# The convolution module over ctx in steps beside the first layer's feed-forward part, and modulation rows beside both attentions

## The chip, the cores and the metric

The kernel runs on one core of a Trainium2 chip. The metric is the device time of one execution in microseconds, lower is better. The engines are named as in the profile: PE is TensorE's matmul, PEld its weight load, DVE is VectorE, ACT is ScalarE, POOL is GpSimd, SP is SyncE, which here only issues DMAs.

## The reference

Two blocks follow one another, in float32. The first has two layers over x (512 tokens, 1024 features): a latent attention and a stick-breaking attention of 4 heads each, whose outputs are merged under sigmoid gates, and a feed-forward part with 2816 hidden features and a causal convolution of width 3. The second block has two layers over x and over ctx (256 tokens): a conformer convolution module in the first, an attention with axial rotary positions in the second, and a gated feed-forward part in each. ctx enters only in the second block, and nothing of x flows into it before the attention. Each layer is modulated by vectors that come from a condition.

```python
def first_block(x, c, ...):
    for l in range(2):
        mod = silu(c) @ w_ada[l] + b_ada[l]            # six vectors of 1024
        h = rms_norm(x, g_norm1[l]) * (1 + sc1) + sh1
        u = h @ w_in[l] + b_in[l]                      # q, kv, stick q k v, two gates
        merged = sigmoid(gate_mla) * (y_mla @ w_branch_mla[l]) + sigmoid(gate_sb) * (y_sb @ w_branch_sb[l])
        x = x + gt1 * (merged @ w_out[l])
        h = rms_norm(x, g_norm2[l]) * (1 + sc2) + sh2
        a, v = split(causal_conv3(h @ w_up[l]))
        x = x + gt2 * ((silu(a) * v) @ w_down[l])

def conv_module(h, ...):
    a, gt = split(h @ w_pw1 + b_pw1)
    u = depthwise_conv31(a * sigmoid(gt)) + b_dw
    return silu(layernorm(u, ln_g, ln_b)) @ w_pw2 + b_pw2

def second_block(x, c, ctx, c_ctx, ...):
    for i in range(2):
        mod_x, mod_c = silu(c) @ w_mod[i] + b_mod[i], silu(c_ctx) @ w_mod[i] + b_mod[i]
        hx, hc = rmsnorm(x) * (1 + sc_x) + sh_x, rmsnorm(ctx) * (1 + sc_c) + sh_c
        yx, yc = conv_module(hx), conv_module(hc)      # i = 0; the attention where i = 1
        x, ctx = x + g_x * rmsnorm(yx), ctx + g_c * rmsnorm(yc)
        x = x + gf_x * rmsnorm(swiglu(rmsnorm(x) * (1 + scf_x) + shf_x))      # ctx the same where i = 0
```

## The kernel before, in words

Arrays are feature-major: 8 tiles of 128 features by the tokens. Every product of float32 matrices is made of three passes over parts that a tensor engine format holds exactly: hi x hi, lo x hi and hi x lo (`dense`, lines 184 to 186). Weights arrive as chunks of 128 x 1024. `weights` (lines 158 to 169) loads one over SP's queue into `raw`, ACT copies the hi part to `whi` (L165), and DVE takes the difference as `wlo` (L168), or POOL does for every `lo_pool`-th chunk. Each of the three has a ring of three buffers. One chunk is 24 matmuls of 512 columns for x, or of 256 for half of x or for ctx.

A modulation row (`modulation_rows`, lines 292 to 313) makes 128 outputs of a vector times a matrix: a DMA of 512 KB, one DVE instruction of 1024 elements that multiplies with the row of the condition (`crow`, for ctx `ccrow`) and accumulates (L308), and a small read of the accumulator. It either takes its buffer from the ring of `raw` and throws its product into the ring of `whi`, or has buffers of its own where a pool is handed over. Rows run in steps: `side_work(n)` (line 146) takes n steps from a generator where the program calls it, next to a chunk's matmuls.

The order of instructions on each engine is fixed when the program is built, by a scheduler that follows the program roughly and moves what is ready. Each engine then runs its queue in order.

The stages of `first_layer` (from line 667), for each of the two layers: the latent attention; the stick attention's queries, keys (`stick_rows`) and values (`stick_values`); its heads, beside 16 `gate` products (L184 to L186 into `g`); 16 `gated` products (L663: gate times the branch product `br`), the second 8 of which are merged and split (L285); the output projection in halves; the feed-forward part in three parts of 8, 7 and 7 hidden tiles, each an `up` stretch (L740 to L752) and a `dn` stretch (L778), the last one in halves of 256 tokens. In layer 0 the attention has 32 rows of its own second half of modulation, one per step of the products from the stick queries on, and the feed-forward part 48 rows for layer 1. Layer 1's attention has none, and its feed-forward part has 48 rows of the second block's matrix, each against two vectors (96 DVE instructions); ctx is loaded and normed there (`start_ctx`, `ctx_norm`).

`conv_layer` (line 885) then has the gating products of ctx (8 tiles, `glu`, 16 chunks) and of x (16 chunks). The 31-wide convolution over ctx is on DVE: one ACT instruction and 30 DVE taps of 256 elements per tile (L929), 12 taps per ctx tile and 15 at two places per x tile. The convolution over x is on PE: each tile is copied by 16 DMAs into shifted copies (`shifted`) and multiplied by 32 small matrices (L948, `cv`). Layer norms and the second products (`back`) follow, ctx's between those of x; `between` starts the next feed-forward part with ctx between the two halves' norms. That part, `ffn2` (line 840), runs in six parts of 4, 4, 4, 3, 3 and 4 hidden tiles over x and ctx. The tiles with names that end in c or begin with ctx are ctx's.

## Time and profile before

| | us |
|---|---|
| runs, median of 3 (lowest, highest) | 3262.71 (3258.6, 3264.51) |
| span of the profiled execution, first to last instruction | 3256.1 |
| PE busy | 3045.2 (94%) |
| DVE busy | 2118.7 (65%) |
| ACT busy | 1378.8 (42%) |
| POOL busy | 818.3 (25%) |
| 622 copies of hi parts, ACT | 599.0 |
| 433 differences for lo parts on DVE, 189 on POOL | 503.2 and 467.0 |
| HBM read and written | 402.81 and 2.10 MB |

The profile is of one execution, and the span is all that it tells of that execution's time. Busy times are sums over the whole span; the stages differ, and the windows below show them apart. The stages in the trace: attention of layer 0 from 66, its output projection from 366, its feed-forward part from 412 to 788; the same of layer 1 from 817, 1113 and 1160 to 1563; the convolution layer from 1563, with ctx's gating products to 1627, x's loop to 1823, norms, and the second products to 1937; the feed-forward part after it to 2500.

### The profile page before, as it was taken

The page shows a single profiled execution, that of the slowest core. Times are in us where ns is not written, and L with a number is a line of the kernel's source. Part 1 is how long each engine was busy: PE and PEld are TensorE (multiplying, and loading weights), DVE is VectorE, ACT ScalarE, POOL GpSimd, SP SyncE. Part 2 cuts the span into 40 slices and gives each one's busy share as a digit, 9 for nine tenths or more (in the row PEclk, how much of TensorE's full clock was granted, in tenths as well). Part 3 has the DMA queues.
Part 4 walks back from the last instruction along what each step waited for, and adds up shares of the span by engine and source line. Part 5 has one row for each costly group of instructions (what it writes and reads, how often), then busy time and mean ns, then how long its engine had stood idle before and what let it go on. Part 6 is the DMA issues. An engine that isn't in the chain of part 4 may idle for free. (4 is left out here: it accounts for less than half of the span.)

```text
span 3256.1 us, 45125 instructions
## 1 busy us (share of the span) xinstructions
PE 3045.2 (94%) x16916; PEld 2554.5 (78%) x16916; DVE 2118.7 (65%) x3863; ACT 1378.8 (42%) x2523; POOL 818.3 (25%) x618
## 2 busy tenths in 40 slices
PE   6999999999999999999899789999998789999997
PEld 5776888888777787877856589888887667898887
DVE  7654775657543688888997786544549976672326
ACT  4535552335534562324513564222235556553223
POOL 4000223233000222223555352000025621240023
PEclk9999999999999999999999889999999989999998
DMA  6442445654221355554434345333434310243323
GB/s 239 135 138 95 136 168 190 192 179 150 90 72 49 123 174 175 170 188 131 146 111 119 104 136 175 98 110 130 138 106 139 119 44 14 75 143 111 94 97 117
DMA packets 129322, 416.69 MB, mean 128 GB/s; under 512 B 16208, under 2 KB 21840, under 8 KB 129104
## 3 DMA queue, kind: packets, MB, share of 16 engines
q1 hardware_dynamic: 123984, 404.96, 38.5%
q10 hardware_dynamic: 3072, 4.43, 0.5%
q0 software_dynamic: 2048, 4.43, 0.5%
q8 instruction: 133, 2.18, 0.3%
q14 instruction: 85, 0.70, 0.1%
HBM read 402.81 MB, written 2.10 MB: 124 GB/s over the span
## 5 line engine op out<-in xcount | busy, mean ns | idle before, releaser
L165 ACT CAST whi<-raw 128x1024 fp32r<-128x1024 f32 (+4 forms) x622 | 599.0, 966 | 1008.8 <-PE dn L185 299.9
L168 POOL TENSOR_TENSOR wlo<-raw,whi 128x1024 fp32r<-128x1024 f32 (+3 forms) x189 | 467.0, 2472 | 1275.0 <-ACT whi L165 1237.4
L168 DVE TENSOR_TENSOR wlo<-raw,whi 128x1024 fp32r<-128x1024 f32 (+4 forms) x433 | 503.2, 1163 | 284.3 <-ACT whi L165 276.8
L184 PE MATMUL dn<-hi,whi 128*128 128x256 f32 (+1 forms) x1088 | 363.5, 338 | 19.8 <-DVE x L778 13.5
L186 PE MATMUL dn<-hi,wlo 128*128 128x256 f32 (+1 forms) x1088 | 361.5, 336 | 7.6 <-DVE wlo L168 7.5
L185 PE MATMUL dn<-lo,whi 128*128 128x256 f32 (+1 forms) x1088 | 364.5, 336 | 1.7 <-DVE lo L285 1.5
L184 PE MATMUL up<-hh,whi 128*128 128x512 f32 (+1 forms) x800 | 292.1, 367 | 7.2 <-ACT hh L269 7.2
L185 PE MATMUL up<-hl,whi 128*128 128x512 f32 (+1 forms) x800 | 292.5, 366 | 0.3 <-DVE hl L270 0.2
L186 PE MATMUL up<-hh,wlo 128*128 128x512 f32 (+1 forms) x800 | 291.7, 365 | 0.0
L308 DVE SCALAR_TENSOR_TENSOR mjunk<-mraw,crow 128x1024 f32<-128x1024 f32 (+1 forms) x176 | 224.0, 1273 | 39.9 <-PE g L185 21.1
L184 PEld LDWEIGHTS dn<-hi,whi 128*128 128x128 f32 x1088 | 207.3, 191 | 47.9 <-issue 14.0
L186 PEld LDWEIGHTS dn<-hi,wlo 128*128 128x128 f32 x1088 | 206.9, 191 | 32.5 <-DVE wlo L168 9.9
L185 PEld LDWEIGHTS dn<-lo,whi 128*128 128x128 f32 x1088 | 208.8, 192 | 25.0 <-DVE lo L285 2.3
L860 DVE TENSOR_TENSOR s<-s,pv 128x512 f32<-128x512 f32 (+1 forms) x76 | 41.0, 539 | 283.7 <-PE pv L186 278.0
L184 PE MATMUL pa<-hh,whi 128*128 128x512 f32 (+1 forms) x496 | 179.5, 362 | 6.2 <-ACT whi L165 3.4
L185 PE MATMUL pa<-hl,whi 128*128 128x512 f32 (+1 forms) x496 | 178.8, 361 | 2.8 <-DVE hl L270 2.7
L186 PE MATMUL pa<-hh,wlo 128*128 128x512 f32 (+1 forms) x496 | 178.0, 359 | 2.0 <-DVE wlo L168 2.0
L184 PEld LDWEIGHTS up<-hh,whi 128*128 128x128 f32 x800 | 152.4, 191 | 31.4 <-ACT hh L269 7.7
L185 PEld LDWEIGHTS up<-hl,whi 128*128 128x128 f32 x800 | 152.4, 191 | 24.5 <-DVE hl L270 0.8
L186 PEld LDWEIGHTS up<-hh,wlo 128*128 128x128 f32 x800 | 152.3, 191 | 23.8
L186 PE MATMUL pv<-hh,wlo 128*128 128x512 f32 (+1 forms) x432 | 152.7, 353 | 0.2 <-POOL wlo L168 0.2
L184 PE MATMUL pv<-hh,whi 128*128 128x512 f32 (+1 forms) x432 | 152.5, 353 | 0.0
(471 smaller groups left out, 7427.7 us busy)
## 6 DMA issues: line engine op xcount, KB each, us to landing
raw<-in_w SPq DMA_DIRECT2D x148, 512.0 KB, 3.4
raw<-in_w_up SPq DMA_DIRECT2D x100, 512.0 KB, 3.5
mraw<-in_w_modt SPq DMA_DIRECT2D x96, 512.0 KB, 3.6
mraw<-in_w_adat SPq DMA_DIRECT2D x80, 512.0 KB, 3.4
raw<-in_w_pw SPq DMA_DIRECT2D x56, 512.0 KB, 3.5
raw<-in_w_down SPq DMA_DIRECT2D x48, 448.0 KB, 3.5
raw<-in_w_g SPq DMA_DIRECT2D x32, 512.0 KB, 3.2
raw<-in_w_out SPq DMA_DIRECT2D x32, 512.0 KB, 3.6
```

The source lines that it names most:

```text
L165: nc.scalar.copy(hi[:, :n], raw[:, :n])
L168: eng.tensor_tensor(lo[:, :n], raw[:, :n], hi[:, :n], op=ALU.subtract)
L184: mm(out, lhsT=hi[:, k, :], rhs=xh[:, cols], start=(k == 0), stop=False)
L185: mm(out, lhsT=hi[:, k, :], rhs=xl[:, cols], start=False, stop=False)
L186: mm(out, lhsT=lo[:, k, :], rhs=xh[:, cols], start=False, stop=(k == n - 1))
L308: behind(nc.vector.scalar_tensor_tensor(junk, raw, 1.0, v, op0=ALU.mult, op1=ALU.mult, accum_out=d[:, f : f + 1]))
L860: nc.vector.tensor_tensor(s, s, pv, op=ALU.mult)
```

## The change

Rows: `side_work` takes two steps in the stick values, gates and gated products, so layer 0's attention holds 80 rows (its own 32 and the 48 for layer 1) and layer 1's attention 80 more (`second_mods`: 48 of the second block for x, then, with `crow` reloaded from a row parked in DRAM, 32 for ctx). The other 16 rows for ctx run in layer 0's feed-forward part. Rows of the second block are loaded once for x and once for ctx, 48 loads more in all. All these rows use the rings of `raw` and `whi`.

ctx: `ctx_conv` is a generator that loads ctx and runs its whole convolution module beside layer 0's feed-forward part, one step per hidden tile or `dn` product: 24 weight chunks, the 240 taps (now L983), the norm before and the layer norm; its output goes to DRAM (`parked`). Layer 1's feed-forward part loads ctx and that output again (`late`) and makes the two norms after the module. `conv_layer` has only x left. ctx's first four hidden tiles of the next feed-forward part are made in it (`fill`): one before x's loop, one before its last convolution, two between the layer norms of the halves. POOL takes no lo parts there any more.

```diff
@@ stick_values, gate, gated
-        core.side_work(1)
+        core.side_work(2)
...
@@ first_layer
-            core.side_work(100)
...
             if part == 0:
-                next_mod(fp)
+                steps = beside(fp)
...
-                core.side_work(2)
-                if k1 == NF and i == k0 + 4:
-                    core.side_work(100)
-                    early()
+                next(steps, None)
             last = k1 == NF
+            if last:
+                for _ in steps:
+                    pass
...
                     else:
-                        core.side_work(1)
+                        next(steps, None)
...
+def ctx_conv(core, fp, T, st, mod_steps, parked):
...
+    for k in range(KD):
+        nc.sync.dma_start(out=T.x[k], in_=a["ctxT"][k])
+    for n in range(EARLY_MODS):
+        for _ in range(-(-16 // EARLY_MODS)):
+            next(mod_steps, None)
+        yield
...
+    for k in range(KD):
+        st.squares(core, T.x[k], k)
+    pre_norm(core, st, 0, norm_gain(core, 0, 0))
+    yield
+    taps = (15,) + tuple(j for j in range(31) if j != 15)
+    for m in range(KD):
+        u = fp.tile([P, C + 30], F32, tag="uc", name="uc", bufs=3)
+        glu(core, lambda: fp.tile([P, S], F32, tag="up", name="sgc", bufs=4), st, m, u, core.at_psum)
+        yield
+        for n, j in enumerate(taps):
+            src = u[:, j : j + C]
+            if n == 0:
+                nc.scalar.activation(T.y[m], src, AF.Identity, bias=core.col("b_dw", m), scale=wdv[:, m, 15:16])
+            else:
+                nc.vector.scalar_tensor_tensor(T.y[m], src, wdv[:, m, j : j + 1], T.y[m], op0=ALU.mult, op1=ALU.add)
+            if n in EARLY_TAPS:
+                yield
+        summed(core, T.y, total, m)
+    layer_norm(core, mean_mat, st, total)
+    yield
+    for m in range(KD):
+        pointwise_back(core, st, m, core.at_psum, squares=False)
+        nc.gpsimd.dma_start(out=parked[m], in_=T.y[m])
+        if m % 2:
+            yield
...
@@ conv_layer
-        core.lo_pool = CONV_LO
-        core.side = taps_dve(us)
-        for m in range(KD):
-            u = up.tile([P, C + 30], F32, tag="uc", name="uc", bufs=KD)
-            glu(T, m, u)
-            us.append(u)
-            core.side_work(CONV_C)
+        next(fill, None)
         ready = []
...
-            core.side_work(CONV_X)
             ready.append(shifted(m, u))
-            if m == KD - 1:
-                back(T)
             if len(ready) > CONV_AHEAD:
                 taps_pe(m - CONV_AHEAD, *ready.pop(0))
-            core.side_work(CONV_X)
...
+        next(fill, None)
         for r in ready:
...
-        pre(T)
-        layer_norm(A, total)
-        between()
-        layer_norm(B, total)
+        layer_norm(core, mean_mat, A, total)
+        for _ in fill:
+            pass
+        layer_norm(core, mean_mat, B, total)
...
@@ emit
-                core.side = core.modulation_rows(a["w_adat"][0], [crow], bias0, [mod], [48], 16)
+                core.side = chain(core.modulation_rows(a["w_adat"][0], [crow], bias0, [mod], [48], 16),
+                                  core.modulation_rows(a["w_adat"][1], [crow], core.colrange("b_ada1"), [mods[1]], [48]))
...
+            def second_mods():
+                yield from mod_rows(0, [crow], [modx[0]], [48])
+                nc.sync.dma_start(out=crow, in_=parked_row.partition_broadcast(P))
+                yield from mod_rows(0, [crow], [modc[0]], [48], 16)
...
+            def late(fp):
...
                 for k in range(KD):
                     nc.sync.dma_start(out=T.x[k], in_=a["ctxT"][k])
+                    nc.sync.dma_start(out=T.y[k], in_=parked[k])
+                for _ in range(LATE_STEPS):
+                    yield
                 for k in range(KD):
+                    st.squares(core, T.y[k], k)
+                yield
+                post_norm(core, st, 2, norm_gain(core, 0, 1))
+                yield
+                T.h = halves_of(T.room(F32R))
+                pre_norm(core, st, 3, norm_gain(core, 0, 2))
...
+            def fill():
+                for f in range(NBUF2):
+                    ffn2_up(core, None, 0, f, [st], {"c": made[f]})
+                    if f in FILLS:
+                        yield
```

Places in the order of instructions. The first is DVE in layer 0's attention, among the gated products of the second branch (`br` is the product, `gate` the gate's tile, `lo` half of the merged tile's split, `wlo` the next chunk's lo part). Before:

```order
L663 TENSOR_TENSOR gate<-gate,br 128x512
L168 TENSOR_TENSOR wlo<-raw,whi 128x512
L285 TENSOR_TENSOR lo<-gate,hi 128x256 x2
L663 TENSOR_TENSOR gate<-gate,br 128x512
L168 TENSOR_TENSOR wlo<-raw,whi 128x512
L285 TENSOR_TENSOR lo<-gate,hi 128x256 x2
```

The same place in the change, where `mjunk` and a column of `mod` are a row's outputs:

```order
L308 SCALAR_TENSOR_TENSOR mjunk,mod_106<-mraw,crow 128x1024
L285 TENSOR_TENSOR lo<-gate,hi 128x256 x2
L308 SCALAR_TENSOR_TENSOR mjunk,mod_106<-mraw,crow 128x1024
L663 TENSOR_TENSOR gate<-gate,br 128x512
L168 TENSOR_TENSOR wlo<-raw,whi 128x512
L308 SCALAR_TENSOR_TENSOR mjunk,mod_106<-mraw,crow 128x1024
L285 TENSOR_TENSOR lo<-gate,hi 128x256 x2
```

Two rows have come between one gated product and the next; PE's order is the same in both kernels here.

The second is DVE at the first `dn` stretch of layer 0's feed-forward part (`dn` is the down product, `x_78` and so on x's tiles). Before, with one row per product:

```order
L308 SCALAR_TENSOR_TENSOR mjunk,mod_106<-mraw,crow 128x1024 x2
L778 SCALAR_TENSOR_TENSOR x_78<-dn,mod_105,x_78 128x512
L308 SCALAR_TENSOR_TENSOR mjunk,mod_106<-mraw,crow 128x1024
L778 SCALAR_TENSOR_TENSOR x_79<-dn,mod_105,x_79 128x512
L168 TENSOR_TENSOR wlo<-raw,whi 128x1024
L308 SCALAR_TENSOR_TENSOR mjunk,mod_106<-mraw,crow 128x1024
L778 SCALAR_TENSOR_TENSOR x_80<-dn,mod_105,x_80 128x512
```

In the change (`uc` is a gated tile of ctx, `early_4514` the output tile that its taps sum into):

```order
L778 SCALAR_TENSOR_TENSOR x_78<-dn,mod_105,x_78 128x512
L168 TENSOR_TENSOR wlo<-raw,whi 128x1024
L907 SCALAR_TENSOR_TENSOR uc<-pa,cols,sgc 128x256
L168 TENSOR_TENSOR wlo<-raw,whi 128x1024
L983 SCALAR_TENSOR_TENSOR early_4514<-uc,wdv,early_4514 128x256 x7
L778 SCALAR_TENSOR_TENSOR x_79<-dn,mod_105,x_79 128x512
L983 SCALAR_TENSOR_TENSOR early_4514<-uc,wdv,early_4514 128x256 x9
```

Runs of taps have taken the place of the rows, and the chunks of the module's own products add their lo parts.

The third is PE at the end of layer 1's feed-forward part, where the convolution layer begins (`pa`, `pg` gating products, `ctx_hl` ctx's normed input). Before, ctx's gating products follow the last `dn`:

```order
L184 MATMUL dn<-hi,whi 128x256
L185 MATMUL dn<-lo,whi 128x256
L186 MATMUL dn<-hi,wlo 128x256
L184 MATMUL pg<-ctx_hl,whi 128x256
L185 MATMUL pg<-ctx_hl,whi 128x256
L184 MATMUL pa<-ctx_hl,whi 128x256
```

In the change one hidden tile of ctx's next feed-forward part (`pv`, and a `pa` before it, 48 matmuls) and the last norm's small matmuls (`rb`) stand between it and x's gating products over 512 columns (`hh_86`, x's normed input):

```order
L185 MATMUL pv<-ctx_hl,whi 128x256
L238 MATMUL rb<-mean_col,acc 128x1
L238 MATMUL rb<-mean_col,sqx 128x1
L238 MATMUL rb<-mean_col,acc 128x1
L238 MATMUL rb<-mean_col,sqx 128x1
L186 MATMUL pv<-ctx_hl,wlo 128x256
L243 MATMUL rb<-ident,rs_y 128x128 x2
L184 MATMUL pg<-hh_86,whi 128x512
```

The 384 matmuls of ctx's gating that stood here have gone to layer 0's feed-forward part.

## Rows read from the trace of the kernel before

**Rows 1.** Stage windows: us, busy PE, PEld, DVE, ACT, POOL, clock, DMA share, GB/s.

```profile
66.00:366.00 300.00, 289.40 (x1265) 223.69 (x1264) 174.84 (x392) 143.25 (x340) 23.85 (x29) 0.99 0.37 121
...
412.00:788.00 376.00, 370.56 (x1916) 316.50 (x1915) 244.77 (x377) 156.01 (x228) 120.42 (x67) 0.99 0.54 177
...
817.00:1113.00 296.00, 285.71 (x1264) 221.78 (x1263) 139.59 (x325) 140.67 (x330) 21.68 (x31) 1.00 0.23 72
...
1160.00:1563.00 403.00, 378.97 (x1926) 321.39 (x1924) 340.30 (x510) 164.05 (x249) 124.44 (x69) 0.97 0.53 169
1563.00:1627.00 64.00, 53.24 (x390) 51.84 (x391) 62.87 (x100) 30.26 (x46) 35.70 (x34) 0.89 0.40 134
...
1823.00:1873.00 50.00, 31.75 (x211) 29.43 (x212) 43.66 (x122) 32.87 (x73) 17.07 (x15) 0.76 0.28 85
1873.00:1937.00 64.00, 55.29 (x434) 54.54 (x433) 51.67 (x100) 41.78 (x85) 31.53 (x20) 0.90 0.50 163
```

**Rows 2.** Waits, whole span: who, for whom: us in total, times, longest.

```profile
PE dn L184 <- DVE x L778: 13.5, 5, 6.9
```

**Rows 3.** DVE's groups by shape: count, busy us, mean ns, idle before.

```profile
L168 DVE TENSOR_TENSOR wlo<-raw,whi 128x1024 fp32r<-128x1024 f32 x309 | 394.5, 1278 | 220.8 <-ACT whi L165 217.1
L308 DVE SCALAR_TENSOR_TENSOR mjunk<-mraw,crow 128x1024 f32<-128x1024 f32 x144 | 184.7, 1283 | 6.7 <-DMA mraw<-in_w_modt 5.4 <-DMA mraw<-in_w_adat 0.9
L929 DVE SCALAR_TENSOR_TENSOR yc<-uc,wdv,yc 128x256 f32<-128x256 f32 x240 | 127.6, 598 | 0.7 <-ACT yc L927 0.7
...
L308 DVE SCALAR_TENSOR_TENSOR mjunk<-mraw,ccrow 128x1024 f32<-128x1024 f32 x64 | 87.4, 1365 | 1.0
...
L308 DVE SCALAR_TENSOR_TENSOR mjunk<-mraw,crow 128x1024 fp32r<-128x1024 f32 x32 | 39.3, 1228 | 33.2 <-PE g L185 21.1 <-PE qk L185 5.0 <-PE sbv L194 4.7
...
L308 DVE DVE_READ_ACCUMULATOR mjunk<-mraw,crow 128x1 f32 x176 | 14.4, 82 | 0.0
```

**Rows 4.** Windows, the last stick heads and the gated products of both layers.

```profile
331.00:366.00 35.00, 34.57 (x151) 27.58 (x150) 25.91 (x45) 20.07 (x45) 12.90 (x13) 1.00 0.32 101
1078.00:1113.00 35.00, 34.54 (x151) 27.53 (x150) 25.88 (x45) 20.17 (x45) 16.25 (x21) 1.00 0.41 131
...
292.00:331.00 39.00, 34.43 (x125) 22.34 (x123) 16.46 (x37) 21.22 (x47) 0.00 (x0) 0.96 0.19 61
```

**Rows 5.** DMA issues, whole span: queue, count, KB each, us to landing.

```profile
mraw<-in_w_adat SPq DMA_DIRECT2D x80, 512.0 KB, 3.4
...
raw<-in_w_br SPq DMA_DIRECT2D x32, 256.0 KB, 2.8
```

**Rows 6.** Windows in which one kind of matmul fills PE.

```profile
1877.00:1901.00 24.00, 24.00 (x202) 24.00 (x201) 19.70 (x29) 19.50 (x38) 11.50 (x6) 1.00 0.55 174
1300.00:1350.00 50.00, 50.00 (x221) 41.10 (x220) 38.78 (x52) 17.20 (x22) 13.01 (x6) 1.00 0.51 169
1762.00:1769.00 7.00, 7.00 (x65) 2.04 (x58) 5.62 (x12) 6.35 (x13) 6.18 (x8) 1.00 0.37 83
```

**Rows 7.** Groups of ACT by shape: a load of its function tables.

```profile
L751 ACT ACT_TABLE_LOAD x1 | 1.3, 1283 | 0.0
```

**Rows 8.** Timeline of PE, before layer 1: start, us, instruction, idle before.

```profile
787.93 0.28 PE L186 MATMUL dn<-hi,wlo 128*128 128x256 f32 x1
...
805.52 0.74 PE L192 MATMUL lat<-whi,hh 128*128 128x448 f32 x1 [1.66 <-ACT hh L269]
```

**Rows 9.** Timeline of PE, layer norms of the convolution layer.

```profile
1832.31 0.56 PE L238 MATMUL rb<-mean_col,acc 128*128 128x1 f32 x2 [9.66 <-DVE acc L221]
...
1839.44 0.69 PE L243 MATMUL rb<-ident,rs_y 128*128 128x128 f32 x2 [3.38 <-DVE rs_y L210]
```

**Rows 10.** Timelines of DVE, then of POOL, in the stretch of ctx's taps.

```profile
1602.07 7.93 DVE L929 SCALAR_TENSOR_TENSOR yc<-uc,wdv,yc 128x256 f32<-128x256 f32 x10
...
1611.06 0.47 DVE L929 SCALAR_TENSOR_TENSOR yc<-uc,wdv,yc 128x256 f32<-128x256 f32 x1
...
1606.65 2.67 POOL L168 TENSOR_TENSOR wlo<-raw,whi 128x1024 fp32r<-128x1024 f32 x1 [2.62 <-ACT whi L165]
```

More of the change, by code (lines that the diff above doesn't have):

```diff
@@ L1 @@
 from contextlib import ExitStack
+from itertools import chain
 import numpy as np
@@ L845, in ffn2 @@
         first, last = part == 0, part == len(parts) - 1
-        hid = {b.tag: [core.pair(fp, b.n, "hid" + b.tag, nbuf) for _ in range(k0, k1)] for b in bases}
+        hid = {b.tag: made[b.tag] if first and b.tag in made else
+               [core.pair(pools[b.tag], b.n, "hid" + b.tag, nbuf) for _ in range(k0, k1)] for b in bases}
         core.lo_pool = 2 if first or last else 0
@@ L882, in ffn2, with conv_layer @@
             yield
-    core.lo_pool = 0
-def conv_layer(core, X, A, B, T, post, pre, between):
+def conv_layer(core, X, A, B, post, pre, fill):
     nc, a, tc = core.nc, core.a, core.tc
-    ob1 = COLS["b_pw1"][0]
     UW = S + 32
```

246 lines of the change are left out of this document (123 added, 123 removed).

## The prediction

> **What bounds the kernel now.** I read the windows by stage first. TensorE (PE) is busy over 90% of both attentions and both feed-forward parts, VectorE (DVE) much less, except in the second feed-forward part, where DVE reaches 340.3 of 403 us (84%) [rows 1]. So PE sets the pace, and what differs between the stages is how often it waits. Two pairs of windows price such waits: the two attentions do the same work, with 32 modulation rows in the first and none in the second (300 and 296 us), and the two feed-forward parts do the same matmuls with 48 and with 96 row instructions (376 and 403 us) [rows 1]. The chain from 1563 to 1937 holds the convolution layer; in its norms, 1823 to 1873, PE is busy 31.75 of 50 us at a granted clock of 0.76 [rows 1]. Outside the norms PE's largest wait for DVE comes to 13.5 us in the whole span [rows 2]: today DVE hardly holds PE up, and a stage that gets more DVE work has room for such waits to appear.
>
> **The change, part by part.** PE's work hardly changes: the 24 chunks of ctx leave one stage and enter another. What changes is what DVE does beside it, and the waits.
>
> *A. Gated products.* A row is a DVE instruction of 1228 ns and the read of its accumulator, 82 ns [rows 3]: 1.31 us. Both layers now have two rows per step. In order, from the split of the last stick head on, 21 rows stand among the DVE work of the last 12 gated products, where none stood. That stretch took 35 us in each layer, PE busy 34.5 and DVE 25.9 [rows 4]. With 21 x 1.31 = 27.5 more, DVE has 53.4 us to do in order, and each gated product waits for a split or a product behind a row: 53.4 - 35 = +18 per layer, **+37**. Bounds: if half the rows drifted ahead into the stick heads' idle time, 53.4 - 13.8 - 35 = 5 per layer, so about +10 for both. At the other end is the ring of three raw buffers: a step now loads two rows of 512 KB (3.4 us each from issue to landing) and one chunk of 256 KB (2.8 us) [rows 5], and DVE must have finished with a buffer before the next load. Two rows and a chunk in turn, partly overlapped, are some 5.6 us (2.8 of load, 2 x 1.31 of rows and a little); 12 steps of it are 67 us, +32 per layer, +64. I take 37, since the DVE sum needs no overlap that I have to guess.
>
> *B. The rest of the attentions.* 160 - 32 = 128 new rows, less the 42 of A, are 86. The slope between the two attentions is (300 - 296) / 32 = 0.125 us a row [rows 1]: 11 us. Layer 1's reload of the row vector and the 16 loads of ctx and of the parked output stand in SP's queue between weight chunks: 2 more, **+13**. Bounds: nothing; or all 18 rows that fall in the last stick heads end up in their chain (there DVE has 16.5 of 39 us [rows 4]), 18 x 1.31 = 24 per layer and 6 for SP, +54.
>
> *C. Feed-forward part of layer 0, with the ctx module.* PE gains 24 chunks of 8 x 3 matmuls of 256 columns, 576 in all. In a stretch full of such matmuls 202 took 24 us, 0.119 us each [rows 6]: 68.5 us, and with norms' small matmuls 71. DVE loses 48 rows (1.283 + 0.082 = 1.365 each [rows 3], 65.5) and gains 16 rows (22), 240 taps at 598 ns (143.5), half of the 24 chunks' splits (12 x 1.278 = 15) [rows 3], and by estimate 39 for the norms and 8 for the gating and sums: 244.8 + 162 = 407 us [rows 1]. Against 376 + 71 = 447 us that is 91%. The part with 84% took 403 - 376 = 27 us longer than the one with 65% [rows 1], so I take **+30** of waits for 91%, bounds 5 (taps have no taker that PE waits for soon, unlike rows they need no DMA) and 45. Sum **+101**. SP's queue has 8 more loads of ctx and one of taps; DMA is at 0.54 [rows 1], so they hide. The kernel has 6 more loads of ACT's function tables, 1283 ns each [rows 7], 7.7 us on an engine that is busy 156 of 376 us here [rows 1]: nothing, and if each delayed a chunk's copy by its length, 8, which the upper bound holds.
>
> *D. Feed-forward part of layer 1.* It loses 96 row instructions (48 x 1.365 on one vector, 48 x (1.365 + 0.082) on the other [rows 3]: 135 us of DVE) and gains two norms of ctx, by estimate 28, so DVE falls to 340 - 135 + 28 = 233 us, about 62% of 376, below that of layer 0's part today. It should then take what that one takes: 376 for 403, rounded for the norms **-25** (bounds -15 to -27).
>
> *E. The convolution layer.* What is left of 374 us (1563 to 1937): four hidden tiles of ctx as fill, 4 x 48 x 0.119 = 22.8; x's gating, 16 chunks x 24 x 0.226 (221 matmuls of 512 columns in 50 us) = 87, and 8 x 64 matmuls of the convolution at 0.108 (65 in 7 us) = 55 [rows 6]; the way back, 16 x 24 x 0.119 = 45.7. Together 210.6. Waits: at the start only 48 ctx matmuls (5.7 us) stand between the last down product and x's gating, where the same norm of a half took 17.5 us from 788.0 to 805.5 before layer 1 [rows 8]: 12, and 2 for the lowered clock behind it. In the loop 10 (the shifted copies), the layer norm of the first half 15 (9.66 us and 3.38 us of PE's waits today [rows 9], with a clock that falls), and 19 for the second half's norm, the post norms and their way into the next part. 210.6 + 58 = 268.6: **-105**, bounds -88 and -125. The bounds come from a last wait that is twice as long, and from waits as few as the attentions have.
>
> Taps today run at 598 ns [rows 3], though one alone takes 470: ten of them beside one POOL split of 2.67 us took 7.93 us, 3.2 over their 4.7 [rows 10]. In C every second chunk goes to POOL, as in the convolution layer today, so I keep the mean of 598.
>
> The Trainium skill, "SBUF — State Buffer", section "Who interferes with whom", has it that a DVE instruction with two SBUF inputs and a GpSimd instruction that reads SBUF exclude one another, and that whichever comes second is blocked for the whole of the other. That agrees with [rows 10]: the excess in ten taps is about one POOL split. By that rule the POOL splits are what counts in C, not the taps' mean, and the sum would be 36 instead of 21; how this comes out of the rows is worked out in rival 2.
>
> **Sum.** 37 + 13 + 101 - 25 - 105 = **+21** on the profiled execution. Its span is 3256.1; the page gives no other time for that execution, and the median of the runs, 3262.7, stands 6.6 above it. 3256.1 + 21 + 6.6 = **3284 us**.
>
> **Rivals.**
> 1. *Rows cost the attentions no more than before* (it would be faster). If the scheduler's order leaves DVE enough lead at the gated products, all 128 rows go at the measured slope, 128 x 0.125 = 16 in place of 50: the sum is -13, **3250 us**; with only 5 us of waits in C it is -38, 3225. For it: layer 0 hides 32 rows for 4 us. Against: in those 35 us PE has no idle time at all and DVE has only 9 [rows 4]. It decides where A and B together stay under 50 - 21 - 6.5 = 22 us.
> 2. *DVE and the raw ring are full.* Some 25 of POOL's splits fall in the stretch of C's taps. If each blocks one of them for most of its own length, 1.9 us (about 2.4 less the 0.5 of a tap [rows 10]), that is 47 us where the taps' mean has 240 x 0.128 = 31 in it. DVE then has 424 of 447 us, 95%, and the waits come to their bound of 45: the sum is 36 and the time 3299. With A at its bound of +64 as well it is 21 + 15 + 27 = +63, **3326 us**. For it: [rows 5, 10]. Against: the mean of 598 comes from a stage with POOL splits at a like density.
> 3. *The parts cancel*, about 3263: A at 16 and the rest as above. That is no mechanism of its own but the middle between 1 and my forecast.
>
> That the module isn't moved at all is no rival here: the order shows the taps beside the down products of layer 0.
>
> **How the numbers follow.** What can be told from no change is 0.2%, 6.5 us. My forecast (3269 to 3306) has 0.42, rival 1 has 0.31, rival 2 0.14, rival 3 0.13. The case of rival 2 with C alone, 3299, lies in the forecast's own range and has 0.1 of its 0.42. Faster by over 0.2%: 0.31; within: 0.13; slower: 0.42 + 0.14 = 0.56. The range reaches down into rival 1 and up into the lower half of rival 2: 3234 to 3320. The forecast's own range is 3269 to 3306.
>
> **What would show it.** Right: the last 12 gated products take about 53 us in each layer with DVE near 100% and PE's waits there ending with a split or product of DVE; layer 0's feed-forward part takes about 477 us, layer 1's about 378; from its end to the next part are some 268 us. A is wrong if those stretches stay at 35 to 40 us; C is wrong if the part takes under 455 us (taps are free) or over 490 (rival 2); E is wrong if the convolution layer takes under 250 or over 285. The prediction as a whole is wrong first through A, since its 37 us alone decide the sign.

## The result, and the profile after

The change made the kernel slower: 3344.91 us median of 4 runs (3337.04 to 3351.63), 1.0259 of before with an interval of 1.0240 to 1.0278. I had forecast 3284 with a range up to 3320. The sign was right, the size was not: the profiled execution's span went from 3256.1 to 3335.3 us, +79.2 where the sum said +21. That execution, 3337.04 us, is the fastest of the four and 8 us under their median, so a difference of medians to the change comes out some 8 us larger than the same difference in the traces.

The windows of the changed kernel by stage, in the columns of [rows 1]; the last two are the last 12 gated products of each layer, up to their last matmul:

```profile
66.00:394.00 328.00, 297.60 (x1262) 223.96 (x1260) 231.70 (x491) 145.07 (x342) 29.50 (x31) 0.98 0.58 185
443.00:940.00 497.00, 455.94 (x2513) 392.37 (x2512) 403.55 (x657) 216.40 (x329) 163.19 (x103) 0.97 0.41 132
970.00:1302.00 332.00, 300.37 (x1263) 225.09 (x1262) 232.29 (x488) 144.66 (x332) 27.32 (x25) 0.97 0.61 193
1350.00:1734.00 384.00, 377.18 (x1944) 322.62 (x1942) 234.43 (x345) 166.52 (x260) 124.27 (x78) 0.98 0.34 109
1734.00:1998.00 264.00, 236.04 (x1538) 171.43 (x1538) 125.61 (x253) 100.38 (x182) 67.46 (x105) 0.93 0.45 128
1998.00:2592.00 594.00, 552.48 (x3316) 492.35 (x3316) 323.94 (x586) 181.16 (x328) 83.77 (x60) 0.96 0.36 117
2592.00:3012.00 420.00, 380.37 (x2507) 318.24 (x2506) 309.22 (x633) 243.67 (x470) 159.51 (x116) 0.97 0.27 86
336.00:390.00 54.00, 40.90 (x144) 27.40 (x143) 46.82 (x81) 19.05 (x43) 17.55 (x14) 0.94 0.68 217
1244.00:1299.00 55.00, 41.23 (x144) 27.51 (x144) 46.76 (x82) 19.45 (x44) 17.60 (x14) 0.94 0.74 234
```

Taken from the start of each stage's first matmul to the next one's, and for A to the end of its last matmul, the time went here:

| term | forecast | measured |
|---|---|---|
| A, last 12 gated products, both layers (34.3 and 34.4 us to 54.4 and 54.9) | +37 | +41 |
| B, rest of the two attentions (all of them: 300 to 328, 296 to 332) | +13 | +24 |
| C, feed-forward part of layer 0 (376 to 498) | +101 | +121 |
| D, feed-forward part of layer 1 (404 to 383) | -25 | -21 |
| E, convolution layer (373 to 264) | -105 | -109 |
| the feed-forward part after it (564 to 594), axial attention after that (432 to 420) | 0 | +18 |
| output projections and the norm between the layers | 0 | +5 |
| sum | +21 | +79 |

Between the last gated product and the output projection PE now waits 3.5 us in layer 0 and 2.9 in layer 1 for the projection's first copy, where it went straight on before:

```profile
PE o L184 <- ACT whi L165: 3.5, 1, 3.5
```

These waits stand under B. The windows of [rows 4] run to the projection; up to there the stretch is 57.8 us in both layers (34.2 before), so A is +47 and B +17 by that measure.

D and E came as forecast in number, and A in size; the runs below show what A is made of. Most of the miss is in three places: C by 20, the feed-forward part that the sum left out by 18, B by 11.

### The profile page after: what moved, and what is told of

Same layout as the page of the kernel before. It is cut to its first block, busy times and chain, and to the rows that moved or that the text cites. A ratio compares the mean times of both kernels' runs of the same rounds, so it can differ in the third digit from the quotient of the medians.

```text
span 3335.3 us, 45309 instructions
## 1 busy us (share of the span) xinstructions
PE 3062.9 (92%) x16916; PEld 2554.5 (77%) x16916; DVE 2126.7 (64%) x3885; ACT 1391.3 (42%) x2529; POOL 760.2 (23%) x606
## 4 chain that ended last, share of the span: by engine, by line
PE 67%; DVE 18%; ACT 5%; DMA 4%; issue 4%; POOL 1%; ACTq 0%; DVEq 0%; SPq 0%; POOLq 0%
PE dn L186 4%; PE dn L184 4%; PE dn L185 4%; PE up L185 3%; PE up L186 3%; PE up L184 3%; PE pa L184 3%; PE pa L185 3%; PE pa L186 3%; DVE wlo L168 3%; DVE early L983 3%; PE pv L186 3%; PE pv L184 3%; PE pv L185 3%; PE cv L1027 2%
## 5 line engine op out<-in xcount | busy, mean ns | idle before, releaser
L168 DVE TENSOR_TENSOR wlo<-raw,whi 128x1024 fp32r<-128x1024 f32 (+4 forms) x453 | 532.3, 1176 | 364.1 <-ACT whi L165 347.7
L168 POOL TENSOR_TENSOR wlo<-raw,whi 128x1024 fp32r<-128x1024 f32 (+3 forms) x169 | 390.2, 2310 | 1178.7 <-ACT whi L165 1134.1
L186 PE MATMUL dn<-hi,wlo 128*128 128x256 f32 (+1 forms) x1088 | 360.0, 335 | 11.3 <-DVE wlo L168 11.2
L308 DVE SCALAR_TENSOR_TENSOR mjunk<-mraw,crow 128x1024 fp32r<-128x1024 f32 (+1 forms) x208 | 258.1, 1241 | 62.8 <-PE g L185 25.8
L186 PE MATMUL up<-hh,wlo 128*128 128x512 f32 (+1 forms) x800 | 294.1, 369 | 0.9 <-DVE wlo L168 0.5
L186 PEld LDWEIGHTS dn<-hi,wlo 128*128 128x128 f32 x1088 | 205.2, 190 | 36.8 <-DVE wlo L168 14.5
L852 DVE TENSOR_TENSOR s<-s,pv 128x512 f32<-128x512 f32 (+1 forms) x54 | 31.7, 588 | 261.7 <-PE pv L186 257.7
L186 PE MATMUL pa<-hh,wlo 128*128 128x512 f32 (+1 forms) x496 | 179.8, 362 | 7.0 <-DVE wlo L168 7.0
L186 PEld LDWEIGHTS up<-hh,wlo 128*128 128x128 f32 x800 | 154.3, 193 | 26.0 <-DVE wlo L168 1.0
L983 DVE SCALAR_TENSOR_TENSOR early<-uc,wdv,early 128x256 f32<-128x256 f32 x240 | 153.1, 643 | 7.2 <-ACT early L981 1.7
L186 PE MATMUL pv<-hh,wlo 128*128 128x512 f32 (+1 forms) x432 | 152.2, 352 | 0.2 <-POOL wlo L168 0.2
```

The lines of the kernel that those rows point to most:

```text
L168: eng.tensor_tensor(lo[:, :n], raw[:, :n], hi[:, :n], op=ALU.subtract)
L186: mm(out, lhsT=lo[:, k, :], rhs=xh[:, cols], start=False, stop=(k == n - 1))
L308: behind(nc.vector.scalar_tensor_tensor(junk, raw, 1.0, v, op0=ALU.mult, op1=ALU.mult, accum_out=d[:, f : f + 1]))
L852: nc.vector.tensor_tensor(s, s, pv, op=ALU.mult)
L983: nc.vector.scalar_tensor_tensor(T.y[m], src, wdv[:, m, j : j + 1], T.y[m], op0=ALU.mult, op1=ALU.add)
```

## The experiments

Ratios are to the kernel before, timed beside each run; the change itself is 1.0259. The diffs are against the change, or against the kernel before where that is said, and are shortened to the lines that matter; `...` stands for code left out. Stage times are from the traces.

### The ring of ctx's gating tile

The timeline of PE in the changed kernel, at the end of the feed-forward part after the convolution layer (`rb` are the norms' small matmuls, `pa` a gating product of ctx):

```profile
2531.55 0.35 PE L238 MATMUL rb<-mean_col,acc 128*128 128x1 f32 x2 [3.73 <-DVE acc L221]
...
2536.03 0.56 PE L238 MATMUL rb<-mean_col,acc 128*128 128x1 f32 x2 [3.46 <-DVE rs_b L209]
...
2545.36 0.69 PE L243 MATMUL rb<-ident,rs_y 128*128 128x128 f32 x2 [6.96 <-DVE rs_y L210]
2555.49 0.56 PE L238 MATMUL rb<-mean_col,acc 128*128 128x1 f32 x2 [9.44 <-DVE acc L221]
...
2559.75 0.69 PE L243 MATMUL rb<-ident,rs_y 128*128 128x128 f32 x2 [2.42 <-DVE rs_y L210]
2565.20 0.58 PE L184 MATMUL pa<-ctx_hl,whi 128*128 128x256 f32 x1 [4.76 <-ACT hp L850]
```

PE stands idle for 31 of 38 us, and the last wait is for ctx's silu (L850), which now writes a tile named `hp`. In the kernel before it wrote `s` (L858). One line of the change, in a helper that the fill needed, took the tile from the norms' ring of five. Put back wherever the feed-forward part's own pool is there:

```diff
-        s = st.tmp.tile("hp") if fp is None or st.base.tag == "c" else fp.tile(...)
+        s = st.tmp.tile("hp") if fp is None else fp.tile(...)
```

> The change also moved ctx's gating tile (line 849) from its own ring s to hp, the norms' ring of five. Theory S: in the last part of the feed-forward part after the convolution layer ctx's silu then stands behind both halves' norms, PE idles about 31 us from 2527 to 2565, and of the 30 us by which that stage grew 13 come back in the axial projections, which find their input earlier. With the tile back in its own ring: stage 1998 to 2592 goes from 594 to about 564 us, the whole by -18, about 3327 us (1.020 of before). Rival: that order comes from the moved rows or from ctx's missing first step, and nothing changes (3345, 1.026).

Measured: 3327.75 us, 1.0202 (1.0179 to 1.0225). That is 18.6 us less than the change, as theory S had it. The stage is back near its 564 us of before (in the columns of [rows 1]):

```profile
2000.00:2567.00 567.00, 547.81 (x3304) 488.56 (x3305) 315.81 (x552) 173.50 (x311) 81.93 (x57) 0.98 0.38 123
```

### The rows in the attentions

First all rows out of layer 1's attention, with constants in their place:

```diff
-            core.side = second_mods()
+            nc.vector.memset(modx[0], 0.01)
+            nc.vector.memset(modc[0][:, 16:], 0.01)
```

> No rows in layer 1's attention (its 80 rows are left out, constants stand in). If rows are all that made that attention 332 us instead of 296, it falls to 296 and the whole by 36, to about 3309. Rival: the loads of ctx and of the parked output, or the two more stall places, carry a part; then it stays at 305 or more and the whole at 3318 or more.

Measured: 3298.22 us, 1.0114 (1.0092 to 1.0136); that attention took 297 us. The rows are 35 of its +36, and the loads of ctx and of the parked output are left with about one.

Which part of a row costs? Two runs took one part away in the gated products. Short rows:

```diff
-                    behind(nc.vector.scalar_tensor_tensor(junk, raw, 1.0, v, ...))
+                    m = self.row_n      # 128 in the gated products
+                    behind(nc.vector.scalar_tensor_tensor(junk[:, :m], raw[:, :m], 1.0, v[:, :m], ...))
```

> The rows in the gated products multiply 128 of their 1024 elements (seven eighths of those sums are left out); all loads stay whole. Theory D: 21 rows by about 1.1 us leave DVE in each layer's last gated products, so they fall from 57 to about 36 us, -20 each, about 3304. Theory R: the chunk's load still waits its turn in the ring; 50 us or more, at most -7 each, 3330 or more.

and thin loads:

```diff
-            nc.sync.dma_start(out=raw, in_=wt[f])
+            nc.sync.dma_start(out=raw[:, :256], in_=wt[f][:, :256])
+            rep = raw[:, :256].unsqueeze(1).to_broadcast([P, 4, 256])
```

> Rows in the gated products load 256 of their 1024 columns and use them four times (three quarters of those rows' weights are left out); the DVE instruction keeps its 1024 elements. Short rows had taken 22 us of DVE work away and left the last 12 products of a layer at 50 and 52 us, against 54.4 and 54.9 in the change and 34.3 before. Theory L (loads: a step asks for 1.28 MB where it asked for 0.25, at some 230 GB/s that is 5 us by itself): with 0.5 MB per step the stretch falls to what DVE needs, 45 to 48 us in each layer, the whole by -14 to -22, about 3327. Theory D (DVE in order): 53 to 55 us, no change.

Measured: 3314.23 us, 1.0160 (1.0135 to 1.0185) and 3323.96 us, 1.0178 (1.0155 to 1.0201). The last 12 products still took 50.0 and 52.2 us with short rows, 52.9 and 49.8 with thin loads. Up to the projection that is 52.8 and 54.0, and 53.2 and 51.6, for the change's 57.8. No theory gave both: D wanted 36 for the first, L 45 to 48 for the second. The windows, short rows first, layer 0:

```profile
334.00:384.00 50.00, 39.42 (x144) 26.81 (x144) 28.97 (x84) 19.20 (x44) 12.26 (x14) 0.97 0.72 237
```

```profile
335.00:388.00 53.00, 40.57 (x145) 27.75 (x143) 48.76 (x85) 19.57 (x43) 17.47 (x14) 0.94 0.32 105
```

With thin loads DVE is busy 49 of 53 us: its time is a limit, as D has it. But with short rows it is busy 29 of 50 us and the stretch is only 3 to 4 us shorter (4 to 5 up to the projection), so there is a second one. PE's waits in the last 12 products of the changed kernel's layer 0, SP's timeline there, ACT's copies of the same chunks, and DVE's difference of the first of them:

```profile
PE br L184 <- ACT whi L165: 10.6, 8, 2.8
...
PE br L186 <- DVE wlo L168: 2.5, 7, 0.7
```

```profile
359.40 0.33 SPq L162 DMA_DIRECT2D raw<-in_w_br  x1
361.08 2.95 SPq L300 DMA_DIRECT2D mraw<-in_w_adat  x2
365.66 0.33 SPq L162 DMA_DIRECT2D raw<-in_w_br  x1
```

```profile
364.18 0.62 ACT L165 CAST whi<-raw 128x512 fp32r<-128x512 f32 x1 [2.11 <-DMA raw<-in_w_br]
368.78 0.62 ACT L165 CAST whi<-raw 128x512 fp32r<-128x512 f32 x1 [2.13 <-DMA raw<-in_w_br]
```

```profile
364.83 0.80 DVE L168 TENSOR_TENSOR wlo<-raw,whi 128x512 fp32r<-128x512 f32 x1 [0.56 <-ACT whi L165]
```

PE waits for copies, and the copies for loads. A step takes three buffers of a ring of three, so a chunk always gets the slot of the chunk before: its load at 365.66 follows the difference that ended at 365.63, and its own copy comes at 368.78. I call that the turn of the slot: load, copy and difference of each chunk, one after another. Two runs on it. The first gave the rows buffers of their own:

```diff
+            elif self.row_pool:         # open from the first gated product to the last
+                raw = self.row_pool.tile([P, 1024], F32, tag="graw", name="mraw", bufs=2)
```

> Rows that run in the gated products load into two buffers of their own instead of the ring of three raw buffers; their DVE work stays. Theory R (ring): a step allocates three raw buffers of a ring of three, so a chunk's load waits for its predecessor's difference, and the step is load, copy, difference in turn: the last gated products go from 57 us to DVE's own 48 or less in each layer, -9 to -15 each, 3345 to about 3322. Theory D (my forecast's: DVE's time in order): the DVE work is the same, 55 to 58 us, no change.

Measured: 3367.11 us, 1.0331 (1.0302 to 1.0359), the other way. Its buffers lie where the stick attention's tiles were, so SP waited 38.4 us for one of those with everything behind it, the rows came in a bunch, and the last products took 66.8 and 69.4 us. It says nothing on the turn. The second gave the chunks the buffers, in the pool that holds the gates; one buffer of the norms' ring `acc` makes room:

```diff
+        if self.br_pool:                # in the gated products
+            raw = self.br_pool.tile([P, 512], F32, tag="braw", name="raw", bufs=2)
-ACB = 3
+ACB = 2
```

> The branch chunks of the gated products load into two buffers of their own; rows keep the ring of three, and one buffer of the norms' ring acc makes room. Taking 22 us of DVE work or three quarters of the rows' bytes away left the last 12 products at 50 to 53 us. Theory Q (the turn of one slot: with two rows and a chunk per step in a ring of three a chunk always gets the slot of the chunk before, so load, copy and difference follow one another, 4.2 to 4.5 us a step): the chunk now loads a step ahead, the stretch falls from 54 to 48 us or less in each layer, at least -12 in all, about 3332. Rival (rows' loads and DVE work each fill the step about as long as the turn): 52 us or more, no change.

Measured: 3308.88 us, 1.0145 (1.0130 to 1.0161): 37 us less, with all rows, all loads and all DVE work in place. The two attentions gave back 12 and 15 us: 4 in each layer's last 12 products (50.1 and 51.3 us), 3 behind them, where PE no longer waits for the projection, and 4.5 and 8 ahead of them. Window, PE's waits and ACT's, layer 0 (the edit's lines shift the numbers by four: L190 is the change's L186):

```profile
332.00:382.00 50.00, 38.70 (x145) 27.56 (x144) 48.51 (x81) 19.48 (x43) 13.03 (x14) 0.94 0.69 235
```

```profile
PE br L190 <- DVE wlo L172: 10.9, 6, 2.7
PE br L188 <- ACT whi L169: 0.4, 1, 0.4
```

```profile
ACT whi L169 <- DVE mjunk L312: 12.7, 6, 2.5
```

PE's waits for copies are gone; those for differences have grown, on a DVE that is busy 48.5 of 50 us. ACT's copies now wait mostly for rows (12.7 us) and less for the branch chunks' loads (4.9, 16.8 in the change), since the rows still throw their products into the ring of `whi`. So there are two limits side by side: the turn of the slot (50.0 and 52.2 us with short rows, 4.2 to 4.4 a step) and DVE's time (50.1 and 51.3 us here). Taking one away shows the other. That nothing but the turn is left with short rows is inferred from the waits; the rows' loads are still in its load time there.

### Layer 0's feed-forward part

Of its 121 us, 68.5 are the module's 576 matmuls at the forecast's 0.119 us; 53 are left, where the forecast had 32. PE's idle time grew by 36 of them (5.4 of 376 us to 41.1 of 497); the rest is in its busy time, at a mean granted clock of 0.97 for 0.99. Four runs each took one thing away. Taps:

```diff
-            else:
+            elif n < 3:
                 nc.vector.scalar_tensor_tensor(T.y[m], src, wdv[:, m, j : j + 1], T.y[m], ...)
```

> ctx's convolution keeps 2 of its 30 DVE taps per tile (28 of 30 left out). Layer 0's feed-forward part lost 53 us to waits and a lower clock, about 22 of them in the down products and the second up stretch, where the taps stand. Theory T (taps in front of the splits that PE waits for): -22 to -26, layer 0's feed-forward part from 498 to about 474, the whole about 3320. Rival N (the norms' small matmuls in PE's queue cost it): at most -10.

Measured: 3309.17 us, 1.0139 (1.0112 to 1.0166); the part took 471.6 us, 26 less. The layer norm:

```diff
-    layer_norm(core, mean_mat, st, total)
+    for k in range(KD):
+        p = T.y[k]
+        nc.scalar.activation(p, p, AF.Silu, bias=core.col("ln_b", k), scale=core.col("ln_g", k))
+        core.split(..., p, k % 2 == 1)
```

> ctx's layer norm in layer 0's feed-forward part loses mean and variance (left out: the two matmul groups, the subtraction, squares and the rsqrt; gain, silu and split stay). Theory N: its matmuls stand in PE's queue among the up products and wait for DVE, so the third up stretch (780 to 898) gives back about 19 us, the whole about 3326. Rival T: that stretch waits for the same splits anyway, at most -6.

Measured: 3320.92 us, 1.0175 (1.0151 to 1.0199); the third up stretch gave back 12 us, the part 13. The edit takes away the norm's work on DVE too; its matmuls on PE wait where they stand in PE's queue in the changed kernel:

```profile
812.00 1.00 PE L925 MATMUL mu<-early,mean_mat 128*128 128x256 f32 x2 [3.84 <-DVE early L983]
...
826.09 0.59 PE L238 MATMUL rb<-mean_col,acc 128*128 128x1 f32 x2 [4.70 <-DVE acc L221]
```

The rows at its start:

```diff
-        for _ in range(-(-16 // EARLY_MODS)):
-            next(mod_steps, None)
...
+    nc.vector.memset(st.mod[:, :16], 0.01)
```

> The 16 rows for ctx at the start of layer 0's feed-forward part are left out (a constant stands in). Theory: four rows per up product in the ring of three raw buffers hold up the chunks there; the stretch from its start to the first down product goes from 109 to about 101 us, the whole by -8, about 3337. Rival: the loads of ctx and the norm do it, -2 or less.

Measured: 3321.89 us, 1.0178 (1.0156 to 1.0200); the first stretch went from 109 to 101 us, the part by 10.6. The three together are 50 of the 53. But the fourth run left all work in place and only moved it:

```diff
-                core.lo_pool = 2
+                core.lo_pool = 2 if l else 0
```

> POOL takes no lo parts in layer 0's feed-forward part; DVE takes its 47 splits too. Taps take 643 ns on average there, one alone 470. Theory P (POOL's splits block taps): taps fall to about 480 ns, -39 us of DVE, against 61 us of added splits: DVE gets 22 us more to do, and the part is 5 to 15 us longer, about 3353. Rival (a tap is slow for another reason): taps stay above 600 ns, DVE gets 61 us more than it had and would need 465 of 498 us: 20 us or more longer, 3365 and up.

Measured: 3302.63 us, 1.0132 (1.0117 to 1.0147), 41 us less (34 in the trace) where I had expected it slower by either theory; 29 of them in this part (498 to 468). Groups of the part in the changed kernel (columns of [rows 3]), DVE's taps and splits and POOL's splits:

```profile
L983 DVE SCALAR_TENSOR_TENSOR early<-uc,wdv,early 128x256 f32<-128x256 f32 x240 | 153.1, 643 | 7.2 <-ACT early L981 1.7
...
L168 POOL TENSOR_TENSOR wlo<-raw,whi 128x1024 fp32r<-128x1024 f32 x35 | 87.1, 2488 | 177.2 <-ACT whi L165 164.5 <-DVE early L983 7.0 <-issue 5.0
...
L168 DVE TENSOR_TENSOR wlo<-raw,whi 128x1024 fp32r<-128x1024 f32 x46 | 60.3, 1310 | 33.4 <-ACT whi L165 33.3
```

and without POOL's splits, with the window of the part:

```profile
L983 DVE SCALAR_TENSOR_TENSOR early<-uc,wdv,early 128x256 f32<-128x256 f32 x240 | 118.6, 512 | 3.1
L168 DVE TENSOR_TENSOR wlo<-raw,whi 128x1024 fp32r<-128x1024 f32 x79 | 98.9, 1253 | 36.4 <-ACT whi L165 35.2 <-PE mu L925 0.8
```

```profile
447.00:925.00 478.00, 452.44 (x2538) 393.10 (x2536) 404.21 (x725) 224.29 (x345) 53.71 (x64) 0.98 0.42 141
```

DVE took over POOL's 47 splits (35 of this shape, 12 narrower) and was busy 404.2 us, where it had been 403.6. What the splits added, about 57 us (35 at 1.25, 12 at 1.10), its other instructions gave back: the taps 34.5, others the rest. PE hardly waited for a split on POOL itself; it waited for copies and for DVE's splits behind other work (PE's waits in the part, the change; DVE's `wlo` in all 11.0 us, 2.6 without POOL's splits):

```profile
PE dn L186 <- DVE wlo L168: 5.8, 4, 2.8
...
PE up L186 <- POOL wlo L168: 0.3, 1, 0.3
```

One tap beside one POOL split in the changed kernel, DVE's timeline, then POOL's:

```profile
591.05 2.62 DVE L983 SCALAR_TENSOR_TENSOR early<-uc,wdv,early 128x256 f32<-128x256 f32 x1
```

```profile
590.00 3.38 POOL L168 TENSOR_TENSOR wlo<-raw,whi 128x1024 fp32r<-128x1024 f32 x1 [3.42 <-ACT whi L165]
```

The tap, 0.47 us alone [rows 10], ends 0.3 us after POOL's split. The same edit in the kernel before, where this part has 48 rows and no taps:

```diff
-                core.lo_pool = 2
+                core.lo_pool = 2 if l else 0
```

> The kernel before, with POOL taking no lo parts in layer 0's feed-forward part, where it has 48 rows and no taps. If POOL's splits cost a part time by themselves (2.5 us each where DVE needs 1.25), it gets faster by 5 us or more, 0.998 or less; if their cost in the change came from blocking the taps, before stays within 5 us (0.9985 to 1.0015) or gets slower, since DVE has room (245 of 376 us) but gains nothing.

Measured: 3259.54 us, 0.9993 (0.9983 to 1.0003): nothing. DVE took 35 splits over there and went from 244.8 to 264.2 us, 17 less than they take, so POOL had blocked it about 0.5 us a split; a DVE that is busy two thirds of the time can spare that. The run also bears on a rival, that a split on POOL costs time because it holds its raw buffer twice as long as one on DVE: SP waited 109.3 us for POOL's splits in this part, and losing those waits gained nothing.

### The parts put together

Rows moved, ring mended, the module where the change put it:

```diff
+ROWS_QK, ROWS_G, ROWS_B = (2, 1), (2, 1), (1, 0)       # rows per step, by layer
-    core.side_work(2)                                  # gated
+    core.side_work(0 if br else ROWS_B[l])
...
+            core.side = core.modulation_rows(a["w_adat"][1], [crow], ..., [mods[1]], [48], 16)   # layer 1
+                return chain(mod_rows(0, [c2, cc], [modx[0], modc[0]], [48, 48], 16, pool=fp),   # its feed-forward part
+                             mod_rows(0, [c2], [modx[0]], [16], pool=fp))
```

> The module stays beside layer 0's feed-forward part; the ring of the gating tile is mended, and the rows go where the runs found room: layer 0's attention has 64 (two per step up to the gates, one in the first 8 gated products, none in the last 8; its own 32, 16 for layer 1, and the 16 for ctx), layer 1's 32 in steps before the gated products, layer 1's feed-forward part 48 loads and 80 row instructions in buffers of its own. If the parts measured so far add up: -18 (ring), -20 and -32 (attentions), -10 (rows in layer 0's feed-forward part), +10 to +17 (layer 1's): 3272 to 3282, 1.003 to 1.007 of before, so still not faster. If the parts overlap, 3295 or more.

Measured: 3273.65 us, 1.0035 (1.0023 to 1.0048). The last 12 products took 34.4 us in both layers, the attentions 301 and 295. The parts add up. Then the layer norm with its sums, its rsqrt and its scaling in a step each:

> As the one before it, and ctx's layer norm is spread over three steps of layer 0's feed-forward part instead of one. If its matmuls in PE's queue are what waits there (leaving the norm out gave back 13 us), the third up stretch gets 5 to 10 us shorter, about 3268; if the scheduler places them as it did, nothing changes.

Measured: 3269.19 us, 1.0028 (1.0018 to 1.0038). The third up stretch got 9 us shorter in the trace (122.1 to 112.9), but the two intervals overlap, so the gain in time is not shown. Then POOL's splits out of layer 0's feed-forward part, by the line above:

> The kernel with the rows moved and the layer norm spread (1.0028 of before), and POOL takes no lo parts in layer 0's feed-forward part. With the change's other parts as they were that made this part 29 us shorter (498 to 469) with no more DVE time in all: DVE took 47 splits over, and its taps fell from 643 to 512 ns. If POOL's splits beside the taps are what the part waited for, it does so here too: 488 to about 460 us, the whole by -27, about 3242, 0.994 of before: faster. Rival: part of those 29 us was the 16 rows at its start, which are gone here; -15, about 3254, 0.998.

Measured: 3229.50 us, 0.9903 (0.9886 to 0.9919): faster than before. The part took 455 us, 79 more than before, of which 68.5 are matmuls. And out of layer 1's:

```diff
-                core.lo_pool = 2 if l else 0
+                core.lo_pool = 0
```

> The same, and POOL takes no lo parts in layer 1's feed-forward part either, where 80 row instructions run and no taps. If any POOL split costs DVE as much as it saves, no change or faster by up to 5; if it is the taps beside them (two inputs in SBUF, short, in front of the splits), DVE gets 59 us more in a part where it is busy some 340 of 402 us, and the part is 10 us or more longer.

Measured: 3219.09 us, 0.9866 (0.9847 to 0.9885), the fastest of all. That part went from 406 to 391 us, more than either outcome that I had put down. Its rows went from 1396 and 1425 ns to 1237 and 1215, 14 us in all, and the splits of its hidden tiles (`lo<-up,hi`) from 1767 to 684, 21 us. Both parts in this kernel:

```profile
414.00:869.00 455.00, 443.36 (x2509) 387.17 (x2508) 376.26 (x669) 219.26 (x330) 46.79 (x56) 0.98 0.38 124
1241.00:1632.00 391.00, 378.00 (x1938) 321.47 (x1937) 325.23 (x544) 168.83 (x261) 49.99 (x40) 0.98 0.53 174
```

How much of that has the kernel before without the change? The edit alone, in layer 1's part of the kernel before:

```diff
-                core.lo_pool = 2
+                core.lo_pool = 0 if l else 2
```

> The kernel before, with POOL taking no lo parts in layer 1's feed-forward part, where it has 96 row instructions. Without POOL's splits the rearranged kernel's part with 80 of them went from 406 to 391 us, its rows from 1396 and 1425 to 1237 and 1215 ns. If that gain is the rows' alone and has nothing to do with the change, this part goes from 403 to about 390 us and the whole by -13 (0.996). Rival: with 96 of them DVE has no room for 35 more splits (340 of 403 us busy), no gain.

Measured: 3246.40 us, 0.9950 (0.9934 to 0.9967). Its part fell from 403 to 382 us with all 96 row instructions in it. The window, the rows, and the hidden tiles' splits, the latter in layer 1's part of the kernel before, in this run, and in layer 0's part of the kernel before:

```profile
1160.00:1542.00 382.00, 372.68 (x1928) 316.96 (x1928) 331.23 (x547) 165.18 (x250) 46.88 (x35) 0.99 0.54 179
```

```profile
L308 DVE SCALAR_TENSOR_TENSOR mjunk<-mraw,crow 128x1024 f32<-128x1024 f32 x48 | 58.5, 1218 | 3.4 <-DMA mraw<-in_w_modt 3.2
L308 DVE SCALAR_TENSOR_TENSOR mjunk<-mraw,ccrow 128x1024 f32<-128x1024 f32 x48 | 58.4, 1217 | 0.3
```

```profile
L285 DVE TENSOR_TENSOR lo<-up,hi 128x512 fp32r<-128x512 f32 x19 | 36.4, 1915 | 26.9 <-ACT hi L282 26.9
```

```profile
L285 DVE TENSOR_TENSOR lo<-up,hi 128x512 fp32r<-128x512 f32 x19 | 13.5, 710 | 14.3 <-ACT hi L282 14.3
```

```profile
L285 DVE TENSOR_TENSOR lo<-up,hi 128x512 fp32r<-128x512 f32 x19 | 13.2, 693 | 41.4 <-ACT hi L282 41.4
```

In layer 1's part of the kernel before, 16 of the 25 splits of hidden tiles took over 1.8 us; each began while POOL was in a split of a chunk and ended 0.3 to 0.55 us after it. In layer 0's part none did, with as many splits on POOL. These hidden tiles are what the down products multiply. PE's largest wait for DVE, the 13.5 us of [rows 2], was nearly all in this part of the kernel before, and is gone in the run:

```profile
PE dn L184 <- DVE x L778: 13.1, 4, 6.9
```

```profile
PE dn L184 <- DVE x L778: 1.0, 2, 0.5
```

So 0.5% of the 1.34% is there without the change. The rest, 0.8%, is what the rearranged kernel adds. How much of that needs the module's move isn't shown: not run was the kernel before without POOL's splits in its convolution layer, where 22 of them stand up to the end of x's loop, beside ctx's taps: 9 took 3.1 us in the mean and 13 took 3.6.

## Why the prediction was right or wrong, step by step

**Sign, D and E: right in number.** The convolution layer gave 109 us for a forecast of 105, and layer 1's feed-forward part 21 for 25. E's two terms were both off and cancelled, which is luck: in its window PE was busy 236.0 us (mean granted clock 0.93) for my 210.6 of matmuls, and idle 28 for my 58 of waits. The change also took POOL's lo parts out of that layer; their share of the 109 wasn't measured.

**A: right in size, half right in cause.** "DVE has 53.4 us to do in order" gave +37, and 54.4 and 54.9 us gave +41. But DVE was busy 46.8 of 54 us, not all of it, and PE waited mostly for copies. The bound that I had set aside, "the ring of three raw buffers", was the limit that came first. It came at 4.5 us a step, not at my 5.6, and is made of the chunk's own load, copy and difference, not of a load and two rows. DVE's time is the limit right behind it: with the chunks' own buffers the stretch stays at 50 us with DVE at 97%.

**B: mis-sized.** "The slope between the two attentions", 0.125 us a row, gave 13; it was 24, within the bounds of 0 to 54: 17 ahead of the last 12 products and 7 behind them. A slope measured with one row per step was carried over to two per step, where the ring has no slot to spare. The run with the chunks' own buffers gave back 4.5 and 8 us ahead and 3 behind in each layer.

**C: the step that failed most.** The matmuls were right, and DVE's time came close: 407 us forecast, 403.6 measured. What failed is the price of the waits, "The part with 84% took 403 - 376 = 27 us longer than the one with 65%", from which I took +30: it was 53. The pair that it rests on doesn't measure what DVE's load costs. Without POOL's splits the 84% part of the kernel before takes 382 us, 6 more than the other, with the same rows and DVE busy 87% of the time. POOL's splits made most of the 27 us, in front of DVE's instructions: 23 us of DVE's time in the hidden tiles' splits and 12 in the rows. In the changed kernel they stand in front of taps as well. I had the mechanism in [rows 10] and priced it as a rival: 25 blocked taps at 1.9 us, 15 us in the sum. The run without those splits gained 29 in the part; of the 57 us that DVE got back, the taps had 34.5. That is 1.2 us for each of the 47 splits, half of a split's 2.5. The Trainium skill ("SBUF — State Buffer", "Who interferes with whom") has it that a DVE instruction with two SBUF inputs and a GpSimd instruction that reads SBUF exclude one another, and by that rule I had 3299. The trace agrees, by the tap and by the hidden tiles' splits above; my price for it was too low. The two other items hidden in C were the layer norm (13 us in all), which I had counted as DVE work only and which has matmuls waiting in PE's own queue, and the 16 rows (10.6). That these go through the ring as in A is likely, but wasn't tested. The four runs give 79 us for the 53, so what they take away overlaps.

**The feed-forward part after the convolution layer: left out.** The sum put it at nothing. I counted what moved and what was added, and passed over which ring the moved helper takes its tile from. 30 us were lost there, of which 13 came back in the axial projections: +18.

**D: right in number, open in cause.** It rests on the same pair. In the change, without its rows but with POOL's splits, the part takes 383 us with 13 of 25 hidden tiles' splits still blocked; in the kernel before, with all its rows but without POOL's splits, it takes 382. So rows and blocked splits cost the 21 us together, and taking either away gives them back. That DVE fell from 84% to 62% isn't needed for it.

**Rivals.** Rival 1 (rows at the small slope) fell: the attentions cost 64 us, not 16. Rival 2 was nearest, with both of its mechanisms there, the ring in A and the blocked DVE work in C; it gave 3326 and had 0.14. With the 18 us of the other ring that makes 3344, but by errors that cancel: it had A at 64 (41 measured), B at 13 (24) and C at 116 (121).

## What to carry to other kernels

Count a ring in allocations per step: where a step takes as many as the ring has buffers, each load waits for its predecessor's last reader, and neither shorter rows nor smaller loads gave more than 5 of 54 us here. When work moves, look at the buffers that its helpers take as well as at its instructions. And before an engine's load is held against a stage's time, look at what its instructions cost there: two stages that differ in load may really differ in how often another engine blocks them, and busy time counts the blocked time too.

## What the runs showed of the hardware that I had not expected

A split on POOL (2.5 us) cost DVE about 1.2 us of blocked time in a stage full of DVE instructions with two SBUF inputs, as much as the 1.25 us that the same split takes on DVE. Handing 47 splits to POOL there bought DVE nothing (403.6 us busy with, 404.2 without) and cost the stage 29 us. In a stage where DVE was busy two thirds of the time such splits cost nothing that could be measured (0.9993). What they hit depends on where they fall: with 35 splits on POOL in both feed-forward parts of the kernel before, 16 of 25 hidden tiles' splits were blocked in one (1915 ns in the mean) and none in the other (693).

Thinner loads and shorter DVE instructions each took 2 to 5 us from a stretch of 54, since two limits stood within a tenth of each other. What stays open: both were never taken away in one run with the rows in place, so how short the gated products get with two rows per step and neither limit isn't known.
